# Moving the operands of each matrix product 320 bytes apart in SBUF: a two-block fp32 network on one core

## The chip, the core and the metric

The kernel runs on one core of a Trainium2 chip. A core has a tensor engine (PE, TensorE) for matrix products, a vector engine (DVE), a scalar engine (ACT), GpSimd (POOL) and a queue engine (SP) that here issues all large transfers. The engines work on SBUF, a memory of 128 partitions, and TensorE writes its products to PSUM. A product has a stationary operand, which is loaded into the array by a weight load (PEld in the profile), and a moving operand, which is streamed through it (PE).

The metric is the device time of one execution in microseconds (us). Three runs of the kernel before took 2036.65, 2035.52 and 2035.12 us; the median is 2035.52.

## The reference

A sequence of 256 tokens with 1024 features passes through two blocks of two layers each, all in float32. Cut to what matters:

```python
def first_block(x, c, ctx, ...):                 # two layers, modulated by c
    for i in range(2):
        sh1, sc1, g1, sh2, sc2, g2 = split(silu(c) @ w_ada[i] + b_ada[i], 6)
        h = rms_norm(x, norm_mix[i]) * (1 + sc1) + sh1
        y = short_conv(h) if i == 0 else neighbourhood_attention(h, hc)
        x = x + g1 * y
        x = x + g2 * swiglu(rms_norm(x, norm_ffn[i]) * (1 + sc2) + sh2, w_in[i], w_out[i])
    return x                                     # ctx goes the same way through layer 0

def second_block(x, mem, ...):                   # two layers
    for i in range(2):
        x = x + 0.5 * swiglu(rms_norm(x, g), ffn1_w_in[i], ffn1_w_out[i])
        proj = rms_norm(x, mix_g[i]) @ w_in      # i == 0: mLSTM heads, i == 1: window heads
        y = concat(heads(proj), memory_heads(proj, mem))
        x = x + y @ w_out
        x = x + 0.5 * swiglu(rms_norm(x, g), ffn2_w_in[i], ffn2_w_out[i])
    return x
```

The hidden size of each swiglu is 2816. Most of the arithmetic is products of a 1024 or 2816 wide activation with a weight matrix.

## The kernel before, in words

Activations lie transposed: features on the 128 partitions in 8 blocks, tokens along the partition, four bytes each. For precision every operand is split into a high part in the format fp32r and the rest: a product then is three matmuls, high by high, high by low and low by high. The method `mm3` (L242 to L246) issues them in that order; its arguments are the stationary high and low part and the moving high and low part.

Weights come from HBM through `WeightStream` (L67 to L115): units of up to 1024 columns per partition are loaded into five raw buffers `wraw` by SP, then split into `whi` by ACT (L106) and `wlo` by DVE (L107), four buffers each. The order of all units is a list made ahead (`stream_specs`), and each consumer takes the next unit; ACT and DVE work some units ahead of TensorE.

Five kinds of product use them:

- `wstat_unit` (L280 to L287): weights stationary, 256 or 512 columns of the activation moving, through `mm3`. The convolution, the first FFN and parts of the mixers go this way.
- `pair_unit` (L299 to L309): weights stationary; the high and low half of the activation lie side by side in one tile (`x2`, `s2`), so that one matmul with 512 moving columns (L307) does high by both, and one with 256 (L309) does low by high. For a block of 128 outputs, four L307 are followed by four L309. The five later FFNs (`ffn_pairs`) go this way, with PSUM tiles `pg` for the hidden layer and `po` for the output.
- `xstat_steps` (L289 to L297): the other way round, a block of 128 tokens of the activation stationary and 256 weight columns moving. Queries, keys and values of the attention and of the mixers go this way.
- `partial` (L318 to L339): output projections, weights stationary and `oh`/`ol` or `yh`/`yl` moving.
- Inside the attention and the mixers: scores with the queries stationary and the keys moving (L1117, L1786, and `mm3` for the memory heads), and values with `vh`/`vl` stationary and the transposed scores `pth`/`ptl` moving. In mixer A the decay-weighted scores `sdh`/`sdl` are stationary and the values `vh0`, `vh1` moving; a row of these tiles is 320 columns long, 1280 bytes, of which 258 are streamed.

The small rest are transposes against the identity in the tile `kc` (L1069, L1095, L1142, L1818 and others), the modulation (L431 to L434), where the vector `sil` or its split `c4` is stationary with 2 or 4 columns, and the gates of mixer A with 8 columns.

Where the attention and mixers have two strands of work, `weave` lays them into one instruction order by costs written in the code (the numbers that the generators yield); that order is fixed when the kernel is built.

**Where tiles lie.** Pools are stacked from the lower end of SBUF in the order in which they are opened, and a few from the upper end (`side="right"`). Within a pool tiles follow each other, rounded up to 32 bytes. In the kernel before, unused tiles fill up the gaps: `fill0` (96 floats), `fill1`, `fill2` (16), `fill3` (120), and some small tiles are made larger than they need (`gq`, `em`, `gqc`, `qs`, `pi`). With them all large tiles begin on a multiple of 512 bytes in their partition: `X`, `t`, `whi`, `wlo`, `xh`, `xl`, `x2`, `s2`, `oh`, `yh`, `kh`, `qh`, `vh`, `pth` and the others. Their inner blocks are multiples of 512 bytes too, but for the value tiles of mixer A. `kc` begins 32 bytes past a multiple, `c4` 256, `ones` and `mean` 128.

Of the kernel before, what the change touches and what calls it, by code (L numbers as in the profile page):

```python
# [7 lines left out]
F32 = mybir.dt.float32  # L8
# [7 lines left out]
P = 128  # L16
# [50 lines left out]
class WeightStream:  # L67
# [4 lines left out]
    def __init__(self, net, es, specs, raw_bufs, split_bufs, ahead):  # L72
        self.nc = net.nc
        self.specs = specs
        self.ahead = ahead
        self.raw_bufs = raw_bufs
        self.raw_pool = es.enter_context(net.tc.tile_pool(name="wraw", bufs=raw_bufs))
        self.split_pool = es.enter_context(net.tc.tile_pool(name="wsplit", bufs=split_bufs))
        self.loaded = 0
        self.split = 0  # L80
        self.used = 0
        self.raw = []
        self.ready = []
        self.width = 512
# [77 lines left out]
class Net:  # L162
    def __init__(self, tc, a, out, es):
        self.tc = tc
        self.nc = tc.nc
        self.a = a
        self.out = out
        self.es = es
        nc = self.nc
        self.cp = es.enter_context(tc.tile_pool(name="const", bufs=1))  # L170
        self.tp = es.enter_context(tc.tile_pool(name="tmp", bufs=8))
        self.rp = es.enter_context(tc.tile_pool(name="rows", bufs=2))
        self.sp = es.enter_context(tc.tile_pool(name="small", bufs=2))
        self.psum = es.enter_context(ExitStack())
        self.banks(6, 2)

        self.cp.tile([P, 96], F32, name="fill0")
        self.X = self.cp.tile([P, KB, T], F32, name="X")
        self.pk = self.cp.tile([P, NPACK], F32, name="pk")
        self.kc = self.cp.tile([P, NCONST], F32, name="kc")  # L180
        nc.sync.dma_start(self.pk, a["pack"])
        self.ident = self.k("ident")
        self.ones = self.cp.tile([P, P], F32, name="ones")
        nc.vector.memset(self.ones, 1.0)
        self.mean = self.cp.tile([P, P], F32, name="mean")
        nc.vector.memset(self.mean, 1.0 / D)
        self.mod = self.cp.tile([P, 2, 48, 2], F32, name="mod")
        self.modA = self.cp.tile([P, 4, KB, 2], F32, name="modA")
# [836 lines left out]
def attention_block(net):  # L1025

    nc, tc, a = net.nc, net.tc, net.a
# [4 lines left out]
    with ExitStack() as es:  # L1032
        op = es.enter_context(tc.tile_pool(name="attn1", bufs=1))
        heads_pool = es.enter_context(ExitStack())
        ap = heads_pool.enter_context(tc.tile_pool(name="attn", bufs=2))
# [17 lines left out]
        def project(q4):  # L1053
            kh = ap.tile([P, 2, 512], F32R, name="kh", tag="kh")
            kl = ap.tile([P, 2, 512], F32R, name="kl", tag="kl")
            qh = ap.tile([P, 2, T], F32R, name="qh", tag="qh")
            ql = ap.tile([P, 2, T], F32R, name="ql", tag="ql")
            qb = net.main_bank()
            yield from net.xstat_steps(qb, (0, 1), xh, xl, net.take2())
            qr = head_rstd(net, [qb], 8, 64, "qr")  # L1060
            qn = net.tmp()
            head_scale(net, qn, qb, qr[:, 0, :], 8, 64)
            ku = net.take2()
            kb = [net.main_bank()]
            yield from net.xstat_steps(kb[0], (0, 1), xh, xl, ku)
            pt = net.aux_bank()
            for t in range(2):
                for pr in range(2):
                    nc.tensor.transpose(pt[:, pr * T + t * P : pr * T + (t + 1) * P],  # L1069
                                        qn[:, t * T + pr * P : t * T + (pr + 1) * P], net.ident)  # L1070
            net.split(qh, ql, pt.rearrange("p (a t) -> p a t", a=2), gq)
            vb = []
            if q4 == 0:
                vu = net.take2()
                vb.append(net.main_bank())
                yield from net.xstat_steps(vb[0], (0, 1), xh, xl, vu)
                kb.append(net.aux_bank())
            else:
                kb.append(net.main_bank())
            yield from net.xstat_steps(kb[1], (2, 3), xh, xl, ku)  # L1080
            kr = head_rstd(net, kb, 8, 64, "kr")
            kn = []
            for i in range(2):
                kn.append(net.tmp())
                head_scale(net, kn[i], kb[i], kr[:, i, :], 8, 64)
            if q4 > 0:
                vu = net.take2()
                vb.append(net.main_bank())
                yield from net.xstat_steps(vb[0], (0, 1), xh, xl, vu)
            vb.append(net.main_bank())  # L1090
            yield from net.xstat_steps(vb[1], (2, 3), xh, xl, vu)
            for pr in range(2):
                pt = net.aux_bank()
                for t in range(4):
                    nc.tensor.transpose(pt[:, t * P : (t + 1) * P],  # L1095
                                        kn[t // 2][:, (t % 2) * T + pr * P : (t % 2) * T + (pr + 1) * P], net.ident)
                net.split(kh[:, pr, :], kl[:, pr, :], pt, gk)
            vh = ap.tile([P, 4, T], F32R, name="vh", tag="vh", bufs=1)
            vl = ap.tile([P, 4, T], F32R, name="vl", tag="vl", bufs=1)
            for i in range(2):  # L1100
                net.split(vh[:, 2 * i : 2 * i + 2, :], vl[:, 2 * i : 2 * i + 2, :], vb[i].rearrange("p (a c) -> p a c", a=2))
            quarter[q4] = (kh, kl, qh, ql, vh, vl)
            yield 0.9
# [309 lines left out]
def mixer_a(net, x2, acc, gain):  # L1413
    nc, tc = net.nc, net.tc
# [3 lines left out]
    with tc.tile_pool(name="mixa", bufs=1) as mp:  # L1418
# [21 lines left out]
        def gates(rc):  # L1440
# [44 lines left out]
            pm = net.aux_bank()  # L1485
            for t in range(2):
                nc.tensor.transpose(pm[:, 4 * t : 4 * t + 4], M[:, t * P : (t + 1) * P], net.ident[0:4, 0:4])
            em = mp.tile([P, P], F32, name="em")[:, :8].rearrange("p (t g) -> p t g", t=2)
            nc.vector.tensor_tensor(em, pm[:, :8].rearrange("p (t g) -> p t g", t=2), Fc, ALU.add)
            nc.scalar.activation(em, em, AF.Exp, scale=-1.0)  # L1490
            env.update(Gc=Gc, em=em)
# [164 lines left out]
def mixer_b(net, x2, acc, gain):  # L1656
    nc, tc = net.nc, net.tc
    xh, xl = x2[:, :, 0, :], x2[:, :, 1, :]
    net.banks(4, 4)
    with tc.tile_pool(name="mixb", bufs=1) as mp:  # L1660
# [5 lines left out]

        kh = mp.tile([P, 2, T], F32R, name="kh")
        kl = mp.tile([P, 2, T], F32R, name="kl")
        vh = mp.tile([P, 2, 2, 2, P], F32R, name="vh")
        vl = mp.tile([P, 2, 2, 2, P], F32R, name="vl")  # L1670
        qt = [[mp.tile([P, 2, T], F32R, name=f"bq{i}{h}") for h in range(2)] for i in range(3)]
        for z in (vh, vl):
            nc.gpsimd.memset(z.bitcast(F32), 0.0)

        pth = [mp.tile([P, 2, 4 * P], F32R, name=f"pth{i}") for i in range(2)]
        ptl = [mp.tile([P, 2, 4 * P], F32R, name=f"ptl{i}") for i in range(2)]
        for i in range(2):
# [4 lines left out]
        for name in ("b_q", "b_k"):  # L1682
            g = net.p(name)
            rot[name] = []
            for i, src in enumerate((net.cos, net.sin)):
# [1 line left out]
                for d0 in (0, 8):  # L1687
                    nc.vector.tensor_tensor(tab[:, :, d0 : d0 + 8], src, g[:, None, d0 : d0 + 8].to_broadcast([P, 2, 8]), ALU.mult)
                rot[name].append(tab)
        gqc = mp.tile([P, 112], F32, name="gqc")[:, :1]  # L1690
        nc.vector.tensor_scalar(gqc, net.p("b_qc"), 0.125, None, ALU.mult)
        gkc = net.p("b_kc")

# [158 lines left out]
def network(tc, a, out, es):  # L1852
    net = Net(tc, a, out, es)
    nc = net.nc
    net.ws = WeightStream(net, es, stream_specs(a), 5, 4, 2)
    net.mk = net.cp.tile([P, 4, T], F32, name="mk")
    net.cp.tile([P, 16], F32, name="fill1")
    net.sp.tile([P, 16], F32, name="fill2", tag="fill2")
    es.enter_context(tc.tile_pool(name="top", bufs=1, side="right")).tile([P, 120], F32, name="fill3")
    net.x_pool = es.enter_context(ExitStack())  # L1860
    net.xp = net.x_pool.enter_context(tc.tile_pool(name="xp", bufs=1))
    net.xh = net.xp.tile([P, KB * 512], F32R, name="xh", tag="xh").rearrange("p (k t) -> p k t", k=KB)
    net.xl = net.xp.tile([P, KB * 512], F32R, name="xl", tag="xl").rearrange("p (k t) -> p k t", k=KB)
    net.ctx_pool = es.enter_context(ExitStack())
    cpool = net.ctx_pool.enter_context(tc.tile_pool(name="ctx", bufs=1))
    net.C = cpool.tile([P, KB, T], F32, name="C")
    net.ada_start()
    conv_block(net)

    def open_x():  # L1870
        net.xp2 = es.enter_context(tc.tile_pool(name="xp2", bufs=1, side="right", reuse_waits="tile"))
        return net.next_x()

    def next_x():
        return net.xp2.tile([P, KB, 2, T], F32R, name="x2", tag="x2")

    net.open_x = open_x
    net.next_x = next_x
    x2, acc = attention_block(net)
    net.rope = net.cp.tile([P, 32], F32, name="rope")  # L1880
    x2, acc = ffn2(net, x2, acc, net.p("mix_g0"), 1, rope=True)
    x2, acc = mixer_a(net, x2, acc, net.p("ffn2_g0"))
    x2, acc = ffn2(net, x2, acc, net.p("ffn1_g1"), 0)
    x2, acc = ffn2(net, x2, acc, net.p("mix_g1"), 1)
    x2, acc = mixer_b(net, x2, acc, net.p("ffn2_g1"))
    ffn2(net, x2, acc, None, 0, last=True)

# [110 lines left out]
```

## Time and profile before

| | |
|---|---|
| median of three runs | 2035.52 us |
| profiled execution | 2036.04 us |
| its span, first to last instruction | 2034.3 us |
| mean granted TensorE clock | 0.999 |
| matmuls, weight loads | 12454 each |
| ACT busy | 1025.4 us |
| HBM read | 345.68 MB, 170 GB/s over the span |

The page of the profile lists busy time by engine, then groups of instructions by line, engine and operation. In a group the names before the arrow are the output, those behind it the operands; for a matmul the moving one stands first and the stationary one second, and `128*128` are the rows and columns of the array in use. The number after the bar is the group's busy time and the mean duration of one instruction in ns. After the second bar stands how long the engine was idle just before these instructions. Durations of matmuls overlap, since they are pipelined. The timeline lists start, duration and instruction, with equal neighbours merged and counted. A line of the view by windows gives, for a stretch, its length and the busy time and count of instructions of each engine.

### The profile page before, as it was taken

The page shows a single profiled execution, that of the slowest core. Times are in us where ns is not written, and L with a number is a line of the kernel's source. Part 1 is how long each engine was busy: PE and PEld are TensorE (multiplying, and loading weights), DVE is VectorE, ACT ScalarE, POOL GpSimd, SP SyncE. Part 2 cuts the span into 40 slices and gives each one's busy share as a digit, 9 for nine tenths or more (in the row PEclk, how much of TensorE's full clock was granted, in tenths as well). Part 3 has the DMA queues.
Part 4 walks back from the last instruction along what each step waited for, and adds up shares of the span by engine and source line. Part 5 has one row for each costly group of instructions (what it writes and reads, how often), then busy time and mean ns, then how long its engine had stood idle before and what let it go on. Part 6 is the DMA issues. An engine that isn't in the chain of part 4 may idle for free. (4 is left out here: it accounts for less than half of the span.)

```text
span 2034.3 us, 32187 instructions
## 1 busy us (share of the span) xinstructions
PE 2015.0 (99%) x12454; PEld 1785.0 (88%) x12454; DVE 1497.2 (74%) x2626; ACT 1025.4 (50%) x1681; POOL 5.1 (0%) x26
## 2 busy tenths in 40 slices
PE   9999999999999999999999999999999999999999
PEld 6788988888899999888888899998888888989888
DVE  5888767776477779766687668787767776888764
ACT  4433532223356556655455556555545555676552
POOL 0000000000000000000000000000000000000000
PEclk9999999999999999999999999999999999999999
DMA  8656365667353334565666564556566656425654
GB/s 262 215 186 190 117 199 164 211 220 246 119 171 115 104 104 126 162 188 182 186 188 184 184 188 125 156 175 188 182 185 192 187 177 187 139 79 176 187 177 134
DMA packets 319273, 348.84 MB, mean 171 GB/s; under 512 B 12624, under 2 KB 307664, under 8 KB 319120
## 3 DMA queue, kind: packets, MB, share of 16 engines
q1 hardware_dynamic: 319120, 346.78, 55.5%
q8 instruction: 98, 1.61, 0.3%
q14 instruction: 55, 0.45, 0.1%
HBM read 345.68 MB, written 1.05 MB: 170 GB/s over the span
## 5 line engine op out<-in xcount | busy, mean ns | idle before, releaser
L107 DVE TENSOR_TENSOR wlo<-wraw,whi 128x512 fp32r<-128x512 f32 (+1 forms) x777 | 702.4, 918 | 354.5 <-ACT whi L106 348.4
L106 ACT CAST whi<-wraw 128x512 fp32r<-128x512 f32 (+1 forms) x777 | 609.5, 805 | 692.2 <-issue 183.8
L307 PE MATMUL pg<-x,whi 128*128 128x512 f32 x1408 | 386.1, 395 | 0.5 <-DVE x L256 0.4
L307 PEld LDWEIGHTS pg<-x,whi 128*128 128x128 f32 x1408 | 240.9, 189 | 34.6 <-DVE x L256 2.2
L307 PE MATMUL po<-s,whi 128*128 128x512 f32 x880 | 243.5, 394 | 0.0
L309 PEld LDWEIGHTS pg<-x,wlo 128*128 128x128 f32 x1408 | 216.0, 189 | 29.8
L309 PE MATMUL pg<-x,wlo 128*128 128x256 f32 x1408 | 224.0, 281 | 0.0
L244 PE MATMUL pm<-xh,whi 128*128 128x512 f32 (+1 forms) x576 | 217.8, 380 | 0.5 <-ACT xh L252 0.5
L245 PE MATMUL pm<-xl,whi 128*128 128x512 f32 (+1 forms) x576 | 217.5, 378 | 0.0
L246 PE MATMUL pm<-xh,wlo 128*128 128x512 f32 (+1 forms) x576 | 217.3, 378 | 0.0
L465 DVE SCALAR_TENSOR_TENSOR ada_acc<-wraw,sil,ada_acc 128x1024 f32<-128x1024 f32 x112 | 140.6, 1279 | 41.3 <-DMA wraw<-in_w_ada 40.8
L307 PEld LDWEIGHTS po<-s,whi 128*128 128x128 f32 x880 | 148.9, 189 | 18.4
L309 PEld LDWEIGHTS po<-s,wlo 128*128 128x128 f32 x880 | 137.8, 189 | 20.6
L309 PE MATMUL po<-s,wlo 128*128 128x256 f32 x880 | 143.0, 280 | 0.0
L244 PEld LDWEIGHTS pm<-xh,whi 128*128 128x128 f32 x576 | 108.1, 188 | 21.3 <-ACT xh L252 1.4
L245 PEld LDWEIGHTS pm<-xl,whi 128*128 128x128 f32 x576 | 108.4, 188 | 20.4 <-DVE xl L253 0.9
L246 PEld LDWEIGHTS pm<-xh,wlo 128*128 128x128 f32 x576 | 108.3, 188 | 19.8
L244 PE MATMUL pm<-sh,whi 128*128 128x256 f32 (+1 forms) x352 | 113.9, 324 | 0.0
L246 PE MATMUL pm<-sh,wlo 128*128 128x256 f32 (+1 forms) x352 | 113.6, 323 | 0.0
L245 PE MATMUL pm<-sl,whi 128*128 128x256 f32 (+1 forms) x352 | 113.3, 322 | 0.0
L246 PE MATMUL pm<-whi,xl 128*128 128x256 f32 x352 | 99.7, 283 | 0.0
L307 PE MATMUL pg<-xh,whi 128*128 128x512 f32 x352 | 97.5, 398 | 1.9 <-DVE xh L253 1.9
(442 smaller groups left out, 3413.8 us busy)
## 6 DMA issues: line engine op xcount, KB each, us to landing
wraw<-in_ffn_w_in SPq DMA_DIRECT2D x264, 512.0 KB, 3.6
wraw<-in_ffn_w_out SPq DMA_DIRECT2D x128, 512.0 KB, 3.5
wraw<-in_w_ada SPq DMA_DIRECT2D x96, 512.0 KB, 4.6
wraw<-in_a_w_in SPq DMA_DIRECT2D x28, 512.0 KB, 3.7
wraw<-in_attn_w_qkv SPq DMA_DIRECT2D x24, 512.0 KB, 4.2
wraw<-in_conv_w_in SPq DMA_DIRECT2D x18, 512.0 KB, 4.4
wraw<-in_ffn_w_out SPq DMA_DIRECT2D x28, 256.0 KB, 2.8
wraw<-in_b_w_in SPq DMA_DIRECT2D x14, 512.0 KB, 3.8
```

The lines of the kernel that those rows point to most:

```text
L106: self.nc.scalar.copy(hi[:, cs], raw[:, cs])
L107: self.nc.vector.tensor_tensor(lo[:, cs], raw[:, cs], hi[:, cs].bitcast(F32), ALU.subtract)
L244: mm(ps, ah, bh, start=first, stop=False)
L245: mm(ps, ah, bl, start=False, stop=False)
L246: mm(ps, al, bh, start=False, stop=last)
L307: self.nc.tensor.matmul(pss[c], hi[:, kk, cs], x2[:, done + kk], start=done + kk == 0, stop=False)
L309: self.nc.tensor.matmul(pss[c][:, 0, :], lo[:, kk, cs], x2[:, done + kk, 0, :], start=False, stop=done + kk == nblocks - 1)
L465: nc.vector.scalar_tensor_tensor(accs[v], w, c, accs[v], ALU.mult, ALU.add)
```

## The change

New unused tiles shift whole pools. `fill3` at the upper end shrinks by 320 bytes and a new pool `shift` of 320 bytes is opened at the lower end above the weight buffers. So everything that is opened after it, and everything at the upper end, begins 320 bytes past a multiple of 512: `xh`, `xl`, `C`, `oh`, `ol`, `yh`, `yl`, `s2`, `x2`, `sh`, `sl`, keys, `bias`, the memory's `mvh` and `mvl`. The weight buffers, `X` and the temporaries `t` stay on multiples. Within the attention and mixer B, tiles of 192 bytes (`fill7`, `fill5`) bring queries and values back to multiples of 512, and tiles of 320 bytes (`fill8`, `fill6`) shift the transposed scores again. In mixer A and B the larger `em` and `gqc` bring `sdh`, `sdl` and the tiles of the memory heads back to multiples.

No instruction is added, removed or reordered.

```diff
@@ project, attention @@
             kh = ap.tile([P, 2, 512], F32R, name="kh", tag="kh")
             kl = ap.tile([P, 2, 512], F32R, name="kl", tag="kl")
+            if q4 == 0:
+                ap.tile([P, 48], F32, name="fill7", tag="fill7", bufs=1)
             qh = ap.tile([P, 2, T], F32R, name="qh", tag="qh")
...
             vl = ap.tile([P, 4, T], F32R, name="vl", tag="vl", bufs=1)
+            if q4 == 0:
+                ap.tile([P, 80], F32, name="fill8", tag="fill8", bufs=1)
@@ gates, mixer A @@
-            em = mp.tile([P, P], F32, name="em")[:, :8].rearrange("p (t g) -> p t g", t=2)
+            em = mp.tile([P, 176], F32, name="em")[:, :8].rearrange("p (t g) -> p t g", t=2)
@@ mixer B @@
         kl = mp.tile([P, 2, T], F32R, name="kl")
+        mp.tile([P, 48], F32, name="fill5")
         vh = mp.tile([P, 2, 2, 2, P], F32R, name="vh")
...
+        mp.tile([P, 80], F32, name="fill6")
         pth = [mp.tile([P, 2, 4 * P], F32R, name=f"pth{i}") for i in range(2)]
...
-        gqc = mp.tile([P, 112], F32, name="gqc")[:, :1]
+        gqc = mp.tile([P, 160], F32, name="gqc")[:, :1]
@@ network @@
-    es.enter_context(tc.tile_pool(name="top", bufs=1, side="right")).tile([P, 120], F32, name="fill3")
+    es.enter_context(tc.tile_pool(name="top", bufs=1, side="right")).tile([P, 40], F32, name="fill3")
+    es.enter_context(tc.tile_pool(name="shift", bufs=1)).tile([P, 80], F32, name="fill4")
     net.x_pool = es.enter_context(ExitStack())
```

After it, for weights stationary and activations moving, the moving operand begins 320 bytes past the stationary one, modulo 512. The same holds for queries against keys and values against scores in the attention and mixer B. For activations stationary and weights moving the stationary operand begins 320 bytes past the moving one. Scores of mixer A (`qkh`, `qkl`) have both operands in shifted tiles and keep their distance.

## The prediction

> **What bounds the kernel now.** I read the page first, then what TensorE waits for, then the timeline of TensorE inside three kinds of matrix product, and last the rows of the weight loads.
>
> ```profile
> span 2034.3 us, 32187 instructions
> ...
> PE 2015.0 (99%) x12454; PEld 1785.0 (88%) x12454; DVE 1497.2 (74%) x2626; ACT 1025.4 (50%) x1681; POOL 5.1 (0%) x26
> ...
> L307 PE MATMUL pg<-x,whi 128*128 128x512 f32 x1408 | 386.1, 395 | 0.5 <-DVE x L256 0.4
> ```
>
> TensorE has a matmul in flight for 99% of the span. In the last row the third field is the idle time before 1408 matmuls of L307: 0.5 us. In the table of waits its largest total is as small:
>
> ```profile
> PE pg L307 <- DVE xh L253: 1.9, 2, 1.7
> ```
>
> So the kernel is bound by the pace at which TensorE passes from one matmul to the next. The busy column does not show that pace, because a matmul's 395 ns overlap with its successor; the distance between starts does. In the timeline (start, duration, instruction), first the convolution's L244 to L246 with 512 moving columns, then the mixer's with 256:
>
> ```profile
> 299.50 0.39 PE L246 MATMUL pm<-xh,wlo 128*128 128x512 f32 x1
> ...
> 300.86 0.39 PE L246 MATMUL pm<-xh,wlo 128*128 128x512 f32 x1
> ```
>
> ```profile
> 1250.05 0.28 PE L244 MATMUL pm<-whi,x 128*128 128x256 f32 x1
> ...
> 1251.97 0.28 PE L245 MATMUL pm<-wlo,x 128*128 128x256 f32 x1
> ```
>
> Six steps take 1.36 us, so 226.7 ns each; sixteen take 1.92 us, so 120 ns each. The 256 extra columns cost 106.7 ns, that is 2.4 columns (9.6 bytes of a partition) per ns. What is left, 13.3 ns, is paid once by every matmul, whatever its width. **That fixed charge is all that the change can touch**, since the columns are the same after it.
>
> In the FFN, groups of four L307 (512 columns) and four L309 (256) alternate:
>
> ```profile
> 1105.14 0.63 PE L309 MATMUL pg<-x,wlo 128*128 128x256 f32 x4
> 1105.62 1.09 PE L307 MATMUL pg<-x,whi 128*128 128x512 f32 x4
> 1106.55 0.64 PE L309 MATMUL pg<-x,wlo 128*128 128x256 f32 x4
> 1107.02 1.09 PE L307 MATMUL pg<-x,whi 128*128 128x512 f32 x4
> 1107.95 0.63 PE L309 MATMUL pg<-x,wlo 128*128 128x256 f32 x4
> 1108.42 1.09 PE L307 MATMUL pg<-x,whi 128*128 128x512 f32 x4
> 1109.35 0.28 PE L309 MATMUL pg<-x,wlo 128*128 128x256 f32 x1
> ```
>
> Three groups of eight take 4.21 us, 1403 ns each; the columns alone (4 x 512 + 4 x 256 at 2.4 per ns) take 1280. The charge is 15.4 ns here, and it moves: from 1105.62 to 1106.55 four wide ones take 232.5 ns each, 5.8 more than the same shape above. **One shape at different charges** is my reason to think that two streams of reads get into each other's way, and that how they lie to each other matters.
>
> Which streams? While a matmul streams its moving operand, the weights of the next one are loaded (PEld, 88%). Two rows of loads, 128 and 4 columns wide:
>
> ```profile
> L307 PEld LDWEIGHTS pg<-x,whi 128*128 128x128 f32 x1408 | 240.9, 189 | 34.6 <-DVE x L256 2.2
> L433 PEld LDWEIGHTS pa<-whi,c 128*4 128x4 f32 x32 | 2.7, 84 | 1.3
> ```
>
> 124 columns more take 105 ns, so a load reads about 4.7 bytes of a partition per ns, half as fast as the stream.
>
> **What the load costs the stream.** Two stretches with 256 moving columns and narrow loads: the mixer's gates (8 columns) and the modulation (4 columns).
>
> ```profile
> 1221.00 0.28 PE L244 MATMUL pm<-x,whi 128*8 128x256 f32 x1
> ...
> 1222.05 0.28 PE L244 MATMUL pm<-x,whi 128*8 128x256 f32 x1
> ```
>
> ```profile
> 57.52 0.28 PE L433 MATMUL pa<-whi,c 128*4 128x256 f32 x1
> ...
> 58.43 0.28 PE L433 MATMUL pa<-whi,c 128*4 128x256 f32 x1
> ```
>
> Nine steps in 1.05 us are 116.7 ns; eight in 0.91 us are 113.8. Against 120, a 128-column load beside the stream costs 3.3 ns more than an 8-column one and 6.2 more than a 4-column one. By the code c4 lies 256 bytes past a multiple of 512 and steps by 16, so in the second stretch the stationary operand lies 320 to 368 bytes from the moving one. Full-width transposes, at half the column rate, pay almost nothing:
>
> ```profile
> 648.51 1.04 PE L1142 MATMUL pa<-kc,t 128*128 128x128 f32 x8
> ```
>
> With 0.27 us for the last, seven steps take 0.77 us, 110 ns for 128 columns that stream in 106.7: a charge of 3 ns. So a load is cheap beside a slow stream and dear beside a fast one.
>
> **The change, part by part.** Addresses are not in the trace; I add up the tile sizes of the code. Before, every large tile begins on a multiple of 512 bytes, so both streams begin at the same offset. The load reads 512 bytes in about 107 ns; in that time the stream reads 1024, so it begins level with the load and has lapped it once just as the load ends: two meetings. With the stream 320 bytes ahead, 192 are missing to a lap, which it makes up at 4.9 bytes per ns in about 39 ns: one meeting, in the middle. This is a picture that fits a charge independent of the width, not something that the trace shows.
>
> The matmuls affected are counted by the lines' totals over the span (duration, PE, PEld):
>
> ```profile
> 0.00:2034.30 2034.30, 656.42 (x2060) 390.53 (x2060) 1.00 0.56 171
> ```
>
> ```profile
> 0.00:2034.30 2034.30, 727.13 (x2640) 450.68 (x2640) 1.00 0.56 171
> ```
>
> These are L244 and L307. L245 and L246 stand in the code beside L244 and run as often, and L309 as often as L307: 3 x 2060 + 2 x 2640 = 11,460. Less 24 gate products with narrow weights and 24 scores of mixer A, whose two operands move together, 11,412 change their distance. Where x is stationary and the weights stream (L296), the distance is the same the other way round: also one meeting, after 320 bytes or 65 ns.
>
> The price of one meeting less is not in the trace. Bounds from rows: gain at most 6.2 ns (the 4-column load), loss at most 5.8 ns (wide matmuls of the FFN against those of the convolution), neither excluded. I take a gain of 3.3 ns, the row of the 8-column load, which leaves one short contact per matmul: **11,412 x 3.33 ns = 38 us.** By the two bounds the sum would be 71 us less or 66 us more.
>
> The rest I cost at nothing. The fills and the new pool issue no instruction and wait for nothing. Scores, transposes and modulation are some 800 short matmuls in stretches that wait for other engines. Vector and scalar instructions that read or write shifted tiles might change by some ns; the room for that is
>
> ```profile
> 50.00:250.00 200.00, 199.18 (x1104) 171.84 (x1103) 170.50 (x260) 86.95 (x151) 0.00 (x0) 1.00 0.58 180
> ```
>
> with DVE, the third busy figure, at 170.5 us of 200 in its fullest long stretch; TensorE 1.9% faster leaves it at 87%. If that cover were gone, DVE's 1497 us would have to grow by a third to set the span. Shifted targets of DMAs are C and the bias:
>
> ```profile
> bias<-in_bias SPq DMA_DIRECT2D x32, 128.0 KB, 2.1
> ...
> C<-in_ctxT SPq DMA_DIRECT2D x2, 512.0 KB, 7.0
> ```
>
> The bias is fetched three tiles ahead and hidden by the scores; a tenth on C's landing would be 0.7 us at the start, no more.
>
> The profiled execution took 2036.04 us, 1.74 around its span of 2034.3, and lies 0.5 above the median of 2035.52. 2036.04 - 38.0 = 1998.0, so the median should come to **1997.5 us**.
>
> **The rivals.** *No change*: the 13.3 ns are a fixed cost of changing weights, and offsets don't matter. For it: the gates' eight weight slices begin 0, 32, ... 224 bytes past a multiple, and their pace is even; and in mixer A the second value tile already begins 256 bytes off (its row is 1280 bytes long), with 258 columns:
>
> ```profile
> 1262.00 0.28 PE L244 MATMUL pa<-vh,sdh 128*128 128x258 f32 x1
> ...
> 1262.36 0.28 PE L245 MATMUL pm<-wlo,x 128*128 128x256 f32 x1
> ```
>
> Three steps of 120 ns, where 258 columns and 13.3 ns make 120.8: under 1 ns gained. Against it: the charge of 3 to 15 ns that varies with rate and neighbours. It gives 2035.5. The Trainium skill speaks for this rival: "TensorE: Matmul & The Clock Gate", section "Step-by-step: what each phase is for", says that TensorE reads the moving operand and the next weights through two independent ports, so that loading takes nothing from the running matmul. The steps of 113.8, 116.7 and 120 ns beside narrower and wider loads speak against that rule, and no run here has yet tried it by address alone.
>
> *Slower, in step*: the single meeting now falls in the middle of the load, where the stream has the longest way left beside it. If each stall lets the load catch up again, the two stay side by side for several reads, instead of parting after the start. Its place is every matmul with a full load; its price is the FFN's 5.8 ns, 11,412 x 5.8 = 66 us, so 2101.5 us. It decides as soon as the mean charge passes today's 13.3 (15.4 in the FFN). For it: the alternating FFN, where the streams lie differently from group to group, already pays more than the even sequences.
>
> *Faster, all contact gone*: charge down by the 4-column row's 6.2 ns, 71 us, 1964.5 us. If even the transposes' 3 ns were reached, 10.3 x 11,412 = 118 us, 1917.5 us. For comparison, the same page of the Trainium skill, section "Wait — 56ns, not 53.3ns?", gives 2.5 ns above the column time for back-to-back matmuls; by it the estimate would be 10.8 ns off each, about 1912 us. The transposes agree with it, the full-rate matmuls here don't.
>
> **How the numbers follow.** Forecast 0.45, all contact gone 0.12, no change 0.17, in step 0.26. 0.2% is 4 us, 0.35 ns per matmul, about what a measurement of this kernel can tell. So faster 0.57, same 0.17, slower 0.26. The range begins at 1945, below the 4-column case, which leaves out 0.07; above it takes in no change and the first third of the slower case (2.1 ns more per matmul, 2060), which leaves out about 0.13. The forecast's own range is 1965 to 2025.
>
> **What would show it.** Right: the step in L244 to L246 falls from 226.7 and 120 to about 223.4 and 116.7 ns and an FFN group of eight from 1403 to about 1376; transposes keep their 110, instruction counts stay at 12454, and DVE's and ACT's busy time stays. Steps of 120 and 226.7 after the change mean no change; steps of 123 and more mean in step. If products with weights stationary and those with x stationary part company, the sign of the distance matters, and my picture of one meeting for both is wrong. If the steps fall but the span doesn't, a wait has taken TensorE's place as the bound.

## The result and the profile after

Six runs of the changed kernel took 2019.21 to 2024.41 us, median 2020.79; six of the kernel before 2035.12 to 2036.78, median 2035.95. The ratio is 0.9927, 95% interval 0.9915 to 0.9940: the change saves 15 us. The direction was as forecast, the size was not: 38 us had been expected.

The profiled run is the slowest of the six, 2024.41 us. TensorE's granted clock averaged 0.996 in it, against 0.999 in four other runs of the change (0.997 in the fifth) and in the profiled run before. From the page:

```profile
span 2022.6 us, 32187 instructions
...
PE 2000.2 (99%) x12454; PEld 1768.0 (87%) x12454; DVE 1497.0 (74%) x2626; ACT 1025.1 (51%) x1681; POOL 5.1 (0%) x26
...
L308 PE MATMUL pg<-x,whi 128*128 128x512 f32 x1408 | 383.6, 394 | 0.6 <-DVE x L257 0.4
```

Line numbers are one higher in the classes that follow (L308 and L310 were L307 and L309, L245 to L247 were L244 to L246). Counts are the same, DVE and ACT are as busy as before, and TensorE still has a matmul in flight for 99% of the span. The wait that was longest in its table has hardly grown (the largest total is now 2.5 us, at L1072):

```profile
PE pg L308 <- DVE xh L254: 2.0, 2, 1.7
```

So the time came out of the pace, as the prediction said. The timeline of TensorE in the FFN, as before:

```profile
1094.44 0.62 PE L310 MATMUL pg<-x,wlo 128*128 128x256 f32 x4
1094.90 1.07 PE L308 MATMUL pg<-x,whi 128*128 128x512 f32 x4
1095.81 0.63 PE L310 MATMUL pg<-x,wlo 128*128 128x256 f32 x4
1096.28 1.09 PE L308 MATMUL pg<-x,whi 128*128 128x512 f32 x4
1097.21 0.62 PE L310 MATMUL pg<-x,wlo 128*128 128x256 f32 x4
```

Two groups of eight take 2.77 us, 1385 ns each, where it was 1403. In the convolution, nine steps with 512 columns:

```profile
300.37 0.39 PE L245 MATMUL pm<-xh,whi 128*128 128x512 f32 x1
...
302.43 0.39 PE L245 MATMUL pm<-xh,whi 128*128 128x512 f32 x1
```

2.06 us, 229 ns each, where it was 226.7: these became slower. With 256 columns, first eleven steps of weights stationary, then six of activations stationary:

```profile
1235.74 0.28 PE L245 MATMUL pm<-x,whi 128*128 128x256 f32 x1
...
1237.04 0.28 PE L247 MATMUL pa<-mkh,yl 128*128 128x256 f32 x1
```

```profile
640.11 0.28 PE L247 MATMUL pm<-whi,xl 128*128 128x256 f32 x1
...
640.79 0.28 PE L247 MATMUL pm<-whi,xl 128*128 128x256 f32 x1
```

1.30 us and 0.68 us: 118 and 113.3 ns, where both were 120. (Other stretches with activations stationary run at 118; the mean is below, and the two paces are shown under "Other distances".) Transposes kept their 110 ns, three steps in 0.33 us after 0.27 for the last:

```profile
645.86 0.60 PE L1147 MATMUL pa<-kc,t 128*128 128x128 f32 x4
```

For the whole kernel I took from the trace the distance from each matmul's start to the next, and the mean for each kind, without the steps that hold a wait (over 160 ns for 256 columns, over 260 for 512). The kinds have these numbers and means:

| kind | matmuls | before, ns | after, ns | times the number, us |
|---|---|---|---|---|
| FFN pairs, 512 columns (L308) | 2640 | 232.3 | 230.4 | -5.0 |
| FFN pairs, 256 columns (L310) | 2640 | 118.4 | 115.75 | -7.0 |
| weights stationary, 512 columns | 1920 | 227.0 | 228.95 | +3.8 |
| weights stationary, 256 columns | 2016 | 119.9 | 117.5 | -4.8 |
| activations stationary, 256 columns | 1776 | 119.8 | 115.4 | -7.8 |

The sum is -20.8 us. The profiled spans differ by 11.7. Stretches in which the clock was granted at half cost the matmul steps 1.7 us before and 6.8 after, 5.1 more. The remaining 4.0 lie in steps that hold a wait or belong to other kinds, such as the modulation (+1.7 us), where TensorE is not alone in setting the pace; I did not follow each to its cause.

### The profile page after: what moved, and what is told of

It is laid out like the page before. It is cut to its first block, busy times and chain, and to the rows that moved or that the text cites. A ratio compares the mean times of both kernels' runs of the same rounds, so it can differ in the third digit from the quotient of the medians.

```text
span 2022.6 us, 32187 instructions
## 1 busy us (share of the span) xinstructions
PE 2000.2 (99%) x12454; PEld 1768.0 (87%) x12454; DVE 1497.0 (74%) x2626; ACT 1025.1 (51%) x1681; POOL 5.1 (0%) x26
## 5 line engine op out<-in xcount | busy, mean ns | idle before, releaser
L308 PE MATMUL pg<-x,whi 128*128 128x512 f32 x1408 | 383.6, 394 | 0.6 <-DVE x L257 0.4
L308 PEld LDWEIGHTS pg<-x,whi 128*128 128x128 f32 x1408 | 239.3, 188 | 33.0 <-DVE x L257 2.8
L308 PE MATMUL po<-s,whi 128*128 128x512 f32 x880 | 241.8, 393 | 0.0
L310 PEld LDWEIGHTS pg<-x,wlo 128*128 128x128 f32 x1408 | 213.5, 188 | 29.4
L245 PE MATMUL pm<-xh,whi 128*128 128x512 f32 (+1 forms) x576 | 219.5, 383 | 0.5 <-ACT xh L253 0.5
L310 PE MATMUL pg<-x,wlo 128*128 128x256 f32 x1408 | 219.8, 278 | 0.0
L247 PE MATMUL pm<-xh,wlo 128*128 128x512 f32 (+1 forms) x576 | 217.9, 379 | 0.0
L246 PE MATMUL pm<-xl,whi 128*128 128x512 f32 (+1 forms) x576 | 217.9, 379 | 0.0
L308 PEld LDWEIGHTS po<-s,whi 128*128 128x128 f32 x880 | 148.0, 188 | 17.3
L310 PEld LDWEIGHTS po<-s,wlo 128*128 128x128 f32 x880 | 136.4, 188 | 20.4
L310 PE MATMUL po<-s,wlo 128*128 128x256 f32 x880 | 140.9, 278 | 0.0
L247 PEld LDWEIGHTS pm<-xh,wlo 128*128 128x128 f32 x576 | 108.1, 188 | 21.7
L245 PEld LDWEIGHTS pm<-xh,whi 128*128 128x128 f32 x576 | 107.9, 188 | 21.7 <-ACT xh L253 1.4
L246 PEld LDWEIGHTS pm<-xl,whi 128*128 128x128 f32 x576 | 108.2, 188 | 21.1 <-DVE xl L254 0.7
L245 PE MATMUL pm<-sh,whi 128*128 128x256 f32 (+1 forms) x352 | 113.7, 323 | 0.0
L247 PE MATMUL pm<-sh,wlo 128*128 128x256 f32 (+1 forms) x352 | 112.9, 321 | 0.0
L246 PE MATMUL pm<-sl,whi 128*128 128x256 f32 (+1 forms) x352 | 112.8, 320 | 0.0
L247 PE MATMUL pm<-whi,xl 128*128 128x256 f32 x352 | 98.2, 279 | 0.0
L308 PE MATMUL pg<-xh,whi 128*128 128x512 f32 x352 | 95.9, 394 | 2.0 <-DVE xh L254 2.0
```

The source lines that it names most:

```text
L245: mm(ps, ah, bh, start=first, stop=False)
L246: mm(ps, ah, bl, start=False, stop=False)
L247: mm(ps, al, bh, start=False, stop=last)
L308: self.nc.tensor.matmul(pss[c], hi[:, kk, cs], x2[:, done + kk], start=done + kk == 0, stop=False)
L310: self.nc.tensor.matmul(pss[c][:, 0, :], lo[:, kk, cs], x2[:, done + kk, 0, :], start=False, stop=done + kk == nblocks - 1)
```

## The experiments

The prediction's theory was that two streams of reads meet once instead of twice within 512 bytes, alike for either sign. Its rivals: what matters is where a tile lies by itself; or the signed distance of the two operands, with a period to be found; or nothing of the addresses that TensorE reads, but something that other engines and transfers do beside it.

### Absolute place or distance

`all_shifted` moves everything by 320 bytes, so that all distances stay at zero. In the kernel before:

```diff
-        self.cp.tile([P, 96], F32, name="fill0")
+        self.cp.tile([P, 176], F32, name="fill0")
-    es.enter_context(tc.tile_pool(name="top", bufs=1, side="right")).tile([P, 120], F32, name="fill3")
+    es.enter_context(tc.tile_pool(name="top", bufs=1, side="right")).tile([P, 40], F32, name="fill3")
```

> Every tile, weights and activations alike, begins 320 bytes past a multiple of 512; the distance between the operands of a product is 0 again. Distance theory: the even steps of before come back (226.7 ns with 512 moving columns, 120 ns with 256), time 2036 within 4 us. Rival, absolute position: it is the offset of the moving tile itself that matters, so the products with weights stationary keep the steps of the change (118 ns with 256 columns, 229 with 512) and the time stays near 2021 us.

`apart_64`, `apart_192` and `apart_256` are the changed kernel with S = 64, 192 and 256 bytes in place of 320. In floats, `fill3` has (480 - S)/4, the tiles that move activations and scores S/4, those that bring queries and values back (512 - S)/4, and `em` and `gqc` grow alike. For S = 192:

```diff
-    es.enter_context(tc.tile_pool(name="top", bufs=1, side="right")).tile([P, 40], F32, name="fill3")
-    es.enter_context(tc.tile_pool(name="shift", bufs=1)).tile([P, 80], F32, name="fill4")
+    es.enter_context(tc.tile_pool(name="top", bufs=1, side="right")).tile([P, 72], F32, name="fill3")
+    es.enter_context(tc.tile_pool(name="shift", bufs=1)).tile([P, 48], F32, name="fill4")
...
-                ap.tile([P, 48], F32, name="fill7", tag="fill7", bufs=1)
+                ap.tile([P, 80], F32, name="fill7", tag="fill7", bufs=1)
```

> As the change, but 192 bytes in place of 320: the moving operand leads by 192 where weights are stationary and by 320 where the activation is stationary, the two roles of the change exchanged. Theory that the signed distance decides: products with weights stationary and 256 columns take the mean step that those with x stationary have in the change (about 115 instead of 118 ns), those with x stationary the 118, and since the former are more, the time falls below the change's 2021, by some 5 to 10 us. Rival, my picture of one meeting instead of two: any distance away from 0 is alike, both classes near 118, time 2021 within 4 us.

> As the change, with 64 bytes in place of 320. Picture of meetings: a stream that begins 64 bytes ahead laps the load after 448 bytes, one meeting near the end of the load, so a gain like the change's, 2021 within 6 us. Rival, that operands must lie far apart: 64 is too near, steps of 120 and 226.7 ns and a time of 2036. Signed distance: neither is excluded.

> As the change, with 256 bytes: both classes of products have the same distance, half a period. Picture of meetings: as the change, 2021 within 4 us, and both classes alike. Signed distance: both classes have one and the same mean step with 256 columns. Before, three matmuls of mixer A that lay 256 bytes apart took 120 ns each; if they are typical, 2036.

Measured, with the kernel before at 2038.72 us beside them: `all_shifted` 2037.52 (ratio 0.9996, 0.9987 to 1.0006), `apart_192` 2031.37 (0.9964, 0.9952 to 0.9977), `apart_64` 2021.36 (0.9918, 0.9903 to 0.9933), `apart_256` 2039.01 (1.0004, 0.9995 to 1.0013). The FFN in `all_shifted` and in `apart_256`:

```profile
1104.83 1.09 PE L307 MATMUL pg<-x,whi 128*128 128x512 f32 x4
...
1107.64 1.09 PE L307 MATMUL pg<-x,whi 128*128 128x512 f32 x4
```

```profile
1105.21 1.09 PE L308 MATMUL pg<-x,whi 128*128 128x512 f32 x4
...
1108.01 1.09 PE L308 MATMUL pg<-x,whi 128*128 128x512 f32 x4
```

Two groups take 2.81 and 2.80 us: the old pace in both. So place by itself does not count: everything lies elsewhere, and nothing happens. And 256 bytes apart is as good as none, while 64 is as good as 320, so the period is 256 bytes and not 512: the picture of one lap within 512 bytes is gone. `apart_192` shows the sign. Its FFN runs nearly as fast as that of the change, three groups in 4.16 us or 1387 ns:

```profile
1093.76 0.62 PE L310 MATMUL pg<-x,wlo 128*128 128x256 f32 x4
...
1097.92 0.62 PE L310 MATMUL pg<-x,wlo 128*128 128x256 f32 x4
```

but weights stationary take 115.1 ns with 256 columns and 233.3 with 512, where `apart_64` has 117.3 and 229.0. Its time had been expected 5 to 10 us below that of the change and came out 10 above it: the expectation had left out what the wide products lose.

### Other distances

`apart_32`, `apart_96`, `apart_128` and `apart_224` come from the same edit, with S = 32, 96, 128 and 224.

> As the change, with 32 bytes. If the charge changes smoothly with the distance: half way between 0 and 64, 118.5 ns with weights stationary and 256 columns, 228 ns with 512, about 2028 us. If a fixed lead of reads decides (first read clear of the other stream's first, or not): all of the gain of 64 bytes, about 2021 us, or none, 2036.

> As the change, with 96 bytes: activations lead by 96 where weights are stationary, and trail by 96 (lead by 160 of 256) where the activation is stationary. Smooth: between the figures of 64 and of 128 in both classes. The two classes then give the curve at 96 and 160 at once.

> As the change, with 128 bytes; both classes again have one distance. 256 bytes behaved as 0 and 64 as 320, so the pattern repeats after 256 bytes and 128 is its middle. Theory that the two streams of reads pass through the same 256 bytes in step and the charge falls with the way between them: the farthest point, steps with 256 columns below 115 ns in both classes, and about 2010 us. Rival, that the gain belongs to the neighbourhood of 64 and 192: between 2021 and 2036.

> As the change, with 224 bytes, that is 32 behind. Signed distance, smooth: products with weights stationary between their figures at 192 and at 0: 117.5 ns with 256 columns, 230 ns with 512, time near 2034 us; those with x stationary as the products with weights stationary have at 32. Rival: near 0 means as 0, 2036 and 120 ns.

The kernel before took 2037.13 us beside them. All four are slower than it: `apart_32` 2042.25 (1.0023, 1.0014 to 1.0033), `apart_96` 2056.96 (1.0092, 1.0072 to 1.0113), `apart_128` 2047.05 (1.0044, 1.0029 to 1.0059), `apart_224` 2044.23 (1.0035, 1.0022 to 1.0047). The FFN of `apart_96`:

```profile
1093.68 1.09 PE L308 MATMUL pg<-x,whi 128*128 128x512 f32 x4
...
1097.92 1.09 PE L308 MATMUL pg<-x,whi 128*128 128x512 f32 x4
```

Three groups take 4.24 us, 1413 ns each. The steps of all runs side by side, in ns. "Ahead" is how far the moving operand begins past the stationary one, modulo 256; with activations stationary it is the negative of S, given in brackets:

| run | ahead | FFN group of eight | weights st., 512 | weights st., 256 | activations st., 256 |
|---|---|---|---|---|---|
| before, `all_shifted`, `apart_256` | 0 | 1403 | 227.0 | 119.9 | 119.8 (0) |
| `apart_32` | 32 | 1400 | 233.3 | 116.9 | 118.3 (224) |
| the change, `apart_64` | 64 | 1384 | 229.0 | 117.4 | 115.5 (192) |
| `apart_96` | 96 | 1413 | 233.3 | 119.95 | 118.3 (160) |
| `apart_128` | 128 | 1404 | 232.65 | 118.8 | 118.9 (128) |
| `apart_192` | 192 | 1387 | 233.3 | 115.1 | 117.2 (64) |
| `apart_224` | 224 | 1403 | 233.3 | 118.4 | 117.0 (32) |

The last two columns are one curve: at 32 bytes ahead 116.9 and 117.0, at 64 117.4 and 117.2, at 128 118.8 and 118.9, at 192 115.1 and 115.5, at 224 118.4 and 118.3, whichever operand the weights are. What counts is how far the moving operand leads the stationary one, with its sign. Wide triples are best at distance 0 and worse at every other tried; the FFN gains at 64 and 192 and nowhere else by more than 3 ns in 1403. Signed distance is the theory that holds so far, without a simple curve: the smooth one had 2028 us for `apart_32`, 2010 for `apart_128` and 2034 for `apart_224`, and missed all three.

The means hide something. In the profiled run of the change, products with activations stationary keep one distance (192 ahead) but run at two paces. The stretch at 640 us shown above takes 113.3 ns a step; another takes 2.12 us for eighteen steps, 118 ns each:

```profile
1239.01 0.28 PE L245 MATMUL pm<-whi,x 128*128 128x256 f32 x1
...
1241.13 0.28 PE L245 MATMUL pm<-whi,x 128*128 128x256 f32 x1
```

Such a pace can last: one stretch runs 105 steps at 118 (624.5 to 636.8 us). Over that whole run 54% of these steps take 112 to 114 ns and 37% take 116 to 118; in `change_again`, the same kernel, 48% and 44%. At 64 ahead (weights stationary, the same two runs) only 7% and 13% take 112 to 114. So the distance decides which paces occur and how often, but not the pace of a single stretch. What picks it stays open.

The Trainium skill, "TensorE: Matmul & The Clock Gate", section "Step-by-step: what each phase is for", has TensorE read the moving operand and the next weights through two independent ports, so that loading takes nothing from the running matmul. These runs disagree: the same work, on the same engines, goes from 2021 to 2057 us by the distance of the two operands alone.

### A finer step, and the best of each

`fine_48_80` and `fine_16_208` are `apart_64` with only the operands of the FFN pairs moved: `x2` to 48 bytes and `s2` to 80, then to 16 and 208. (The `x2` of the first of these FFNs lies in the tile `xh` and stays at 64; its groups are not counted below.) `mixed` gives each kind a distance that the table likes: `xh` and `xl` level with the weights through the first layer (convolution and FFN) and 64 ahead from the attention on, `oh`, `ol`, `yh` and `yl` 192 ahead; its diff is against the change, whose other distances of 320 bytes become 64 in it. `change_again` is the change itself, run beside it on the same chip. `fine_16_208` differs from the diff below only in the starts of its two slices, 52 and 36 floats in place of 60 and 4.

```diff
@@ fine_48_80 @@
-        return net.xp2.tile([P, KB, 2, T], F32R, name="x2", tag="x2")
+        return net.xp2.tile([P, KB * 512 + 64], F32R, name="x2", tag="x2")[:, 60 : 60 + KB * 512].rearrange("p (k a t) -> p k a t", k=KB, a=2)
-        s2 = hp.tile([P, HB, 2, T], F32R, name="s2")
+        s2 = hp.tile([P, HB * 512 + 64], F32R, name="s2")[:, 4 : 4 + HB * 512].rearrange("p (k a t) -> p k a t", k=HB, a=2)
@@ mixed @@
-    net.xh = net.xp.tile([P, KB * 512], F32R, name="xh", tag="xh").rearrange("p (k t) -> p k t", k=KB)
+    wide = [net.xp.tile([P, KB * 512 + n], F32R, name=t, tag=t) for t, n in (("xh", 64), ("xl", 64))]
+    view = lambda t, o: t[:, o : o + KB * 512].rearrange("p (k t) -> p k t", k=KB)
+    net.xh, net.xl = view(wide[0], 48), view(wide[1], 48)
+    net.xh1, net.xl1 = view(wide[0], 0), view(wide[1], 0)
...
+        op.tile([P, 32], F32, name="fill9")
+        op.tile([P, 32], F32, name="fill10")
```

> From the kernel with 64 bytes: the FFN's x2 at 48 bytes and s2 at 80, so 16 bytes to either side of 64, in one kernel (pg and po products). If 64 is a minimum of a smooth curve: FFN groups of eight at 1388 to 1395 ns in both, between their figures at 64 (1385) and at 32 or 96 (1400 and 1413). If the position matters in steps of 32 or 64 bytes: 48 as 32 or as 64, 80 as 64.

> The FFN's x2 at 16 bytes and s2 at 208. Smooth: pg groups of eight between 1403 (at 0) and 1400 (at 32), po groups between 1387 (at 192) and 1403 (at 224). Steps of 64 bytes: 16 as 0, 1403; 208 as 192, 1387.

> Each class of product at the distance that was best for it in the series: 0 for the 512-column products of the first block (xh, xl; 226.7 instead of 229 ns, 1536 matmuls, 3.5 us), 192 for the output projections (oh, yh; 115 instead of 117.5 ns, 768 matmuls, 1.9 us), 64 elsewhere (which behaves as 320). If the charge depends on the distance alone, class by class, the time is 5 us below the change: 2015.5, ratio 0.990. Rival, that the classes' figures carry over only in company with the rest of the layout: no difference to the change, 2021.

> The change itself once more, beside the next kernel on one chip: ratio 0.9927 to the kernel before, within its interval.

A single run each gave 2032.83 us for `fine_48_80` and 2028.43 for `fine_16_208`, with the kernel before at 2037.45. Their groups of eight take 1400 ns at 48 bytes, 1403 at 80, 1393 at 16 and 1409 at 208, against 1384 at 64. Moving 16 bytes away from 64, to either side, thus loses nearly all of the FFN's gain. Neither the smooth curve nor steps of 32 or 64 bytes gives all four figures.

`change_again` took 2020.42 us (0.9915, 0.9902 to 0.9929), `mixed` 2017.26 (0.9902, 0.9888 to 0.9915). Its runs, 2016.76 to 2017.98, all lie below those of the change, 2019.38 to 2024.84; the gain of 3.2 us was forecast at 5. In the convolution of `mixed`, eighteen steps take 4.08 us, 226.7 ns each, as in the kernel before:

```profile
298.79 0.39 PE L245 MATMUL pm<-xh,whi 128*128 128x512 f32 x1
...
302.87 0.39 PE L245 MATMUL pm<-xh,whi 128*128 128x512 f32 x1
```

Over the kernel, wide triples go from 228.95 to 227.45 ns (1920 of them: 2.9 us) and narrow ones from 117.5 to 116.8 (2016: 1.4 us). The first figure is most of the 3.8 us by which the change had slowed the wide products.

### TensorE alone

`bare_scan` leaves the network out. It loads one set of operands, copies them on ACT, and then TensorE runs matmuls only, with no other engine and no transfer beside them until the end. At each of 16 distances, in steps of 16 bytes, it runs triples with 512 columns (`pa`), triples with 256 (`pb`) and FFN groups of four and four (`pc`). Four more stretches (`pd` to `ph`) let both operands alternate between 0 and 64 bytes, so that the moving operand is level either with its own weights or with those being loaded for the next matmul.

```diff
+    def crossed(name, n, own):
+        for c in range(2):
+            ps = pool.tile([P, 512], F32, name=name, tag="pm")[:, :n]
+            for i in range(24):
+                kk, e = i % 4, i % 2
+                mm(ps, weights(0, kk, c, 16 * e), moving(0, kk, n, 16 * (e if own else 1 - e)), start=i == 0, stop=i == 23)
+    for j in range(16):
+        triples512(4 * j)
+        triples256(4 * j)
+        pairs(4 * j)
```

> The network is left out; the kernel only loads four fp32r tiles and multiplies them, and returns its input. For each of 16 distances (0 to 240 bytes in steps of 16) it issues 48 matmuls in triples with 512 moving columns, 48 in triples with 256, and 48 in the FFN's groups of four wide and four narrow; then 4 x 48 in which stationary operands at 0 and at 64 bytes alternate, with the moving operand level with its own stationary operand (so 64 from the one being loaded next) or 64 from its own (so level with the next). Distance alone: the mean steps of the full kernels come back without any other engine at work: 227 ns at 0, 229 at 64, 233 at 192 for 512 columns; 120, 117.3, 115.1 for 256; groups of eight 1403, 1384, 1387 ns. Rival, that the writes of ACT, DVE and the DMAs take part: the curve is flat or another one. Alternating: if the distance to the weights being loaded counts, the level-with-own runs lie near the mean of 64 and 192 (116 ns with 256 columns, 231 with 512) and the others at 120 and 227; if the distance to its own weights counts, the other way round.

The page shows that TensorE was alone:

```profile
PE 440.4 (96%) x2496; PEld 383.9 (84%) x2496; ACT 7.3 (2%) x5; POOL 0.2 (0%) x4
```

In the timeline, three groups of eight at distance 0, at 96 and at 192:

```profile
36.91 1.09 PE L1904 MATMUL pc<-xh,whi 128*128 128x512 f32 x4
...
41.12 1.09 PE L1904 MATMUL pc<-xh,whi 128*128 128x512 f32 x4
...
188.08 1.10 PE L1904 MATMUL pc<-xh,whi 128*128 128x512 f32 x4
...
192.33 1.09 PE L1904 MATMUL pc<-xh,whi 128*128 128x512 f32 x4
...
339.44 1.09 PE L1904 MATMUL pc<-xh,whi 128*128 128x512 f32 x4
...
343.60 1.09 PE L1904 MATMUL pc<-xh,whi 128*128 128x512 f32 x4
```

4.21, 4.25 and 4.16 us: about 1403, 1417 and 1387 ns (means over the stretch are in the table). Then 21 steps with 256 columns at distance 192, and 24 with 512 at distance 240:

```profile
334.34 0.28 PE L1895 MATMUL pb<-xh,whi 128*128 128x256 f32 x1
...
336.72 0.28 PE L1895 MATMUL pb<-xh,whi 128*128 128x256 f32 x1
...
399.18 0.39 PE L1886 MATMUL pa<-xh,whi 128*128 128x512 f32 x1
...
404.62 0.39 PE L1886 MATMUL pa<-xh,whi 128*128 128x512 f32 x1
```

2.38 us and 5.44 us: 113.3 and 226.7 ns. Mean steps at all distances, in ns, for triples without the first eight steps of each stretch. (The first stretch of wide triples ran partly at the half clock and is left out; its last 24 steps take 226.7.)

| ahead | 512 | 256 | group of eight | | ahead | 512 | 256 | group of eight |
|---|---|---|---|---|---|---|---|---|
| 0 | - | 120.0 | 1403 | | 128 | 232.6 | 118.7 | 1402 |
| 16 | 231.6 | 116.6 | 1393 | | 144 | 233.3 | 118.7 | 1404 |
| 32 | 233.3 | 116.7 | 1400 | | 160 | 234.2 | 118.7 | 1410 |
| 48 | 233.4 | 118.3 | 1400 | | 176 | 233.3 | 119.3 | 1403 |
| 64 | 228.9 | 117.8 | 1386 | | 192 | 233.3 | 113.3 | 1387 |
| 80 | 231.1 | 119.95 | 1403 | | 208 | 234.7 | 119.15 | 1407 |
| 96 | 233.3 | 120.05 | 1413 | | 224 | 233.4 | 118.4 | 1403 |
| 112 | 231.1 | 113.7 | 1383 | | 240 | 226.7 | 117.3 | 1400 |

At the distances that the network had too, its groups of eight agree within 2 ns, and its triples within 2 ns. So the curve belongs to TensorE's own reads; DVE, ACT and DMA are not needed for it. But each distance has one stretch here, so where two paces occur the table shows the one that came up: at 192 it has 113.3 ns, where the network's mean is 115.1. At 112 the steps varied from 113 to 120 ns at first and then settled at 113.3. The four crossed stretches in the timeline:

```profile
423.40 5.78 PE L1913 MATMUL pd<-xh,whi 128*128 128x256 f32 x48
429.02 5.91 PE L1913 MATMUL pe<-xh,whi 128*128 128x256 f32 x48
434.77 11.29 PE L1913 MATMUL pf<-xh,whi 128*128 128x512 f32 x48
445.89 11.36 PE L1913 MATMUL ph<-xh,whi 128*128 128x512 f32 x48
```

In `pd` and `pf` the moving operand is level with its own weights, and 64 or 192 ahead of those being loaded; in `pe` and `ph` it is level with those being loaded. If the load in progress counts, `pd` should run at the mean of 117.8 and 113.3, about 116, `pe` at 120, `pf` at the mean of 228.9 and 233.3, about 231, and `ph` at 227. Measured: 116.5, 119.8, 231.8 and 233.3. So the distance to its own weights does not decide alone, in either width: `pd` would then take 120 and `pf` 227. With 256 columns the means are those that the load in progress would give, but the single steps of `pe` are not: they run from 116 to 130 ns in a repeating pattern, where at distance 0 each takes 120. With 512 the stretch that should have been level, `ph`, ran at 233.3 and not at 227. Which of the two weight tiles counts is therefore not shown.

## Why the prediction was right in its direction and wrong in its size

- *What bounds the kernel*: right. TensorE's pace set the time before and after; waits, counts and the other engines' busy time stayed.
- *The charge beyond the columns is what can be touched*: right. The mean step at 256 columns moves between 113.3 and 120.05 ns when nothing but addresses changes; the columns, by the prediction's rate, are 106.7 of it.
- *Two meetings become one, alike for all shapes and both signs*: wrong. The period is 256 bytes and not 512 (`apart_256` equals the kernel before), the sign matters (115.1 ns at 192 ahead, 117.4 at 64), and wide triples, level before, got slower by 2.0 ns. The text had named the test itself: products with weights stationary and with activations stationary did part company, 117.5 and 115.4 ns.
- *3.33 ns for each of 11,412 matmuls*: **this is the step that failed.** The kinds moved by -1.9, -2.7, +2.0, -2.4 and -4.4 ns; the 15.2 us of the medians are 1.3 ns per matmul. The price came from one row, the gates at 116.7 ns, read as the cost of a wide load against a narrow one. But by the code the narrow rows differ from the 120 ns row in the distance of their operands too: eight slices 0 to 224 bytes past a multiple in the gates, and 320 to 368 bytes in the modulation, which is 144 to 192 ahead modulo 256. A full-width load reaches 113.3 ns at 192 ahead, what I had put down to a 4-column load. Nor is the gates' pace a fixed one. In `apart_128` nine of their steps take 1.02 us, 113.3 ns each:

```profile
1230.39 0.28 PE L247 MATMUL pm<-x,wlo 128*8 128x256 f32 x1
...
1231.41 0.28 PE L247 MATMUL pm<-x,wlo 128*8 128x256 f32 x1
```

By the code the moving operand lies 96, 64, 32 and 0 bytes ahead in these steps, where full loads take 116.7 to 120.05 ns in `bare_scan`. So a narrow load is cheaper there, but its pace does not follow the table of distances, and it says nothing of what a full load saves when it is moved. No row held that price; it was argued, not shown.

- *Right for one kind only*: an FFN group fell from 1403 to 1385 where 1376 was forecast, narrow steps to 117.5 and 115.4 where 116.7 was, and wide triples rose to 229 where 223.4 was. The prediction had 226.7 and 120 in one fence with one charge of 13.3 ns, and the FFN's 15.4 beside them as a sign that the charge moves. It does, and at one distance it moves up for one shape and down for the other: at 192 ahead (`apart_192`), with the prediction's 106.7 and 213.3 ns for the columns, it is 8.4 ns with 256 columns and 20.0 with 512. One charge "whatever its width" fits distance 0, where it was read off, but not these.
- *The rest costed at nothing*: nearly. DVE and ACT kept their times. But of the 20.8 us that the steps gained, about 4 were given back in steps with waits, and 5 in the profiled run to the half clock.
- *The rivals*: "no change" is what a distance of 256 gives, and would have been this change's result had it moved by 256. "Slower, in step" was a real possibility with its price too high: `apart_96` is 19.8 us slower than the kernel before, not 66. The 6.2 ns of "all contact gone" are reached by some stretches with 256 columns at 192 ahead, but nowhere by all kinds at once. The choice of distance decides between these, and the prediction had no row to tell 64 from 96: its picture of one meeting would have promised a gain for both. So the direction was in part luck: of 32, 64, 96, 128, 192 and 224 bytes only 64 and 192 made the kernel faster.

What stays open: what in the memory makes the curve, why it changes within 16 bytes, which of the two weight tiles counts, and what decides between two paces at one distance.

## What to carry to other kernels

Where TensorE runs back to back and bounds the kernel, the distance between the moving and the stationary operand, modulo 256 bytes and signed, is worth some per cent of a step and costs only unused bytes: scan it in a bare sequence of the kernel's own shapes first, with several separate stretches for each distance, then give each kind of product its own. A step read from a trace has more than one cause in it; before its difference to another row is used as a price, look at what else differs, addresses included. And a gain in pace that is found for one shape must be looked up for each, since here the same shift helped 256 columns and hurt 512.

## What the runs showed of the hardware

- The mean distance between starts of full-width fp32r matmuls depends on how far the moving operand lies ahead of the stationary one, modulo 256 bytes: 113.3 to 120.05 ns with 256 columns, 226.7 to 234.7 with 512, 1383 to 1413 for a group of eight, with TensorE alone.
- It is uneven at 16 bytes: 120.05 ns at 96 ahead, 113.7 at 112, 118.7 at 128 (256 columns, one stretch each in `bare_scan`).
- At one distance two paces occur with 256 columns: 113.3 and 118 ns at 192 ahead, each for a whole stretch, in one run of the change.
- The best distance depends on the shape: 192 or 112 for narrow triples (113.3 and 113.7 ns), 0 or 240 for wide ones (226.7), 64, 112 or 192 for the mixed groups (1383 to 1387), by these stretches.
- Narrow loads run otherwise: eight-column gates take 116.7 ns before and 113.3 in `apart_128`, where the moving operand lies 96 to 0 bytes ahead and full-width loads pay 116.7 to 120.05.
- Where both operands lie together makes no difference (`all_shifted` 0.9996, 0.9987 to 1.0006).
